# Weight splits taken off GpSimd and a second block's products shifted by one unit, in the experts of a hybrid decoder layer

## The chip, the cores and the metric

The kernel is one program on one core of a Trainium2 chip. The metric is the device time of one execution in microseconds (us); lower is better. TensorE is written PE in the profile, its weight load PEld, VectorE DVE, ScalarE ACT, GpSimd POOL, SyncE SP. [...]

## The reference, cut to what matters

One layer: attention and a short convolution, a mixture of experts, and an embedding gate. The change lies in the experts. 2048 tokens each choose one of 4 groups by a router, and two of the 8 experts in that group:

```python
def expert_block(args):
    xblk, e = args
    hdn = jax.nn.silu(xblk @ w_gate[e]) * (xblk @ w_up[e])
    return hdn @ w_down[e]
```

A token's two results, weighted, are added to its row. `w_gate` and `w_up` are 1024 x 512 for each of the 32 experts, `w_down` 512 x 1024, all float32.

## The kernel before, in words

*Stages.* `build` runs the input projection, the attention, the output projection with the routing (`mix_out`), the experts (`far_experts`, for tokens past an expert's first 192, then `experts`), and `finish`. Products are made of two float32r parts of each operand: `split` (line 59) writes hi = cast of src on ScalarE (line 65), and lo = src - hi (line 66), on VectorE unless another engine is named. `mm3` (lines 73 to 75) adds hi·hi, hi·lo and lo·hi.

*Weights as a ring.* An expert's weights are 12 units of 128 x 1024: 0 to 3 of `w_gate`, 4 to 7 of `w_up` (two halves of 256 columns, two units each), 8 to 11 of `w_down`. SP loads them into 12 raw buffers in turn (`unit_loads`, line 749). `split_unit` splits the next one into one of 10 pairs `uh`, `ul`; with `pool=True` lo is made on GpSimd. In `block` the call `free` says that the place of a unit is done with, and splits the next in line there (`next_unit`, line 764), which also issues the next load.

*An expert.* Loop over 32 experts, `block(e, more)`: the first 128 tokens ("first block"), and, under a branch on the expert's count, 64 more ("second block", `more`). `prods(j, 0)` multiplies unit j with the first block (6 products of 512 columns, or 12 of 256); `prods(j, 1)` with the second, whose hi and lo rows stand side by side as 128 rows (4 or 8 products, lines 1286 and 1287). `first(j)` and `others(j)` call them and do what follows: after unit 3 the SiLU; after units 5 and 7 a half of the hidden layer (`hidden`: for the first block `u`, line 1300; for the second `half`, which adds its two halves of rows by a ScalarE copy in line 1251 and a VectorE addition in line 1252, and the product of line 1297, tile `sum`); a unit later its transposes on TensorE (`hidden_trans`, line 1307) and their split (`hh`, `hl`; for the second block `hs`). After units 8 and 9 the next expert's tokens are transposed (line 1230). After unit 11 `store` empties the output banks: line 1321 on ScalarE for the first block, `half` again for the second.

*Order.* The schedule is manual: each engine runs its instructions in the order in which the code issues them. The loop is, for j from 1 to 10: `first(j)`, `others(j - 1)`, `free(j in (4, 6))`; then `others(10)`, `others(11)`, `first(11)`. So two units per expert are split with lo on GpSimd, and the second block stays one unit behind the first. The transposes go into a pool of two PSUM tiles, `tr`, used in turn by all transposes of the experts. Banks are six: 0 and 1 for the gate (first and second block), 2 to 5 for `w_up` and then for the outputs.

GpSimd's queue also holds the gathers of tokens (line 1221) at an expert's head and the stores of results (lines 1323 and 1325).

Of the kernel before, what the change touches and what calls it, by code (L numbers as in the profile page):

```python
# [18 lines left out]
DRAM = bass.MemoryType.DRAM  # L19
# [11 lines left out]
EPS = 1e-6  # L31
# rows of the experts' outputs: the first 128 of each expert, then the next 64 of each;
# those past 192 go in blocks of 128 of their own
R1 = E * 128
R2 = R1 + E * 64
FAR = 192
# units of weights on chip, as loaded and split
NRAW, NSPLIT = 12, 10
# [3 lines left out]
# tiles of p @ w_ple_proj that wait until the experts are done  # L42
# [3 lines left out]
def row_bc(ap, n):  # L46
    """A DRAM row of n elements, read by every partition."""
    return bass.AP(tensor=ap.tensor, offset=ap.offset, ap=[[0, 128], [1, n]])


class Kernel:
# [7 lines left out]
    def split(self, hi, lo, src, lo_eng=None, hi_eng=None, later=None):  # L59
        """hi + lo = src, each of them exact in float32r; lo only noted where it is for later."""  # L60
        nc = self.nc
        if hi_eng:
            hi_eng.tensor_copy(hi, src)
        else:
            nc.scalar.activation(hi, src, AF.Copy)  # L65
        f = lambda: (lo_eng or nc.vector).tensor_tensor(lo, src, hi.bitcast(F32), op=OP.subtract)  # L66
        f() if later is None else later.append(f)

    def mm3(self, ps, terms, start=True, stop=True):
        """ps += sum of (ah + al)^T (bh + bl), al^T bl aside."""  # L70
        mm, n = self.nc.tensor.matmul, len(terms)
        for i, (ah, al, bh, bl) in enumerate(terms):
            mm(ps, ah, bh, start=(start and i == 0), stop=False)  # L73
            mm(ps, ah, bl, start=False, stop=False)  # L74
            mm(ps, al, bh, start=False, stop=(stop and i == n - 1))  # L75

    def acc(self, ps, prods):
        """ps = the sum of products."""
        for i, (l, r) in enumerate(prods):
            self.nc.tensor.matmul(ps, l, r, start=i == 0, stop=i == len(prods) - 1)  # L80

    def rsqrt_steps(self, pool, r, v):
        """r = v ** -0.5, from an integer guess and three Newton steps; stops between two of them."""
        V = self.nc.vector
        t = pool.tile([128, r.shape[1]], F32, name="rsq_t", bufs=2)
        ri = r.bitcast(I32)
        V.tensor_scalar(ri, v.bitcast(I32), 1, None, op0=OP.logical_shift_right)
        yield
        V.tensor_scalar(ri, ri, -1.0, float(0x5F3759DF), op0=OP.mult, op1=OP.add)
        for _ in range(3):  # L90
            yield
            V.scalar_tensor_tensor(t, r, -0.5, r, op0=OP.mult, op1=OP.mult)
            yield
            V.tensor_tensor(t, t, v, op=OP.mult)
            yield
            V.scalar_tensor_tensor(r, t, 1.5, r, op0=OP.add, op1=OP.mult)
# [6 lines left out]
    def rms_steps(self, pool, r, ss, n):  # L103
        """r = 1 / sqrt(ss / n + EPS), by columns."""
        v = pool.tile([128, ss.shape[1]], F32, name="rms_v", bufs=2)
        self.nc.vector.tensor_scalar(v, ss, 1.0 / n, EPS, op0=OP.mult, op1=OP.add)
        yield
        yield from self.rsqrt_steps(pool, r, v)
# [62 lines left out]
    def project(self, st):  # L171
        tc, nc, a = self.tc, self.nc, self.a
# [51 lines left out]
        # gains and taps as columns: q 0-2, kv 3-4, taps 5-16 (tap, channel tile)  # L224
# [5 lines left out]
        # rows of the rotary tables: frequency, phase in turns, phase; 64 of cosines, 64 of sines  # L230
# [8 lines left out]
        # sums of every 32nd row  # L239
# [26 lines left out]
        def up_weights():  # L266
            # tiles of 128 columns: 0-3 two heads each without rotation, 4-5 the rotated halves of four heads each
# [176 lines left out]
        def start():  # L444
            """The first tokens' way to the first columns, in the order in which they come."""
# [8 lines left out]
            later = []  # L454
# [81 lines left out]
    def rope_angles(self, f512, pi, rcol):  # L536
        """Angles within a turn, for positions pi, a row's kind given by rcol."""
# [17 lines left out]
        # a turn more or less where the first guess was a little off  # L555
# [10 lines left out]
    def attention(self, st):  # L566
# [32 lines left out]
        def scores(h, g, qi, c):  # L599
            """Scores of 128 queries and 512 keys; with the last of a row's, its softmax."""  # L600
# [70 lines left out]
        def sums(h, g):  # L671
            """1 / the softmax's sums."""
            sm = groups[h, g]["sm"] = wk.tile([128, 4], F32, name="sm")
            nc.vector.tensor_reduce(sm, groups[h, g]["rs"][:, :, :g + 1], axis=AX.X, op=OP.add)
            nc.vector.reciprocal(sm, sm)

        def sums_row(h, g):
            """The same along the free axis, on a head's partitions."""
            G, a0 = groups[h, g], heads[h]["a0"]
            q = nc.sync if (h, g) == hg[-1] else nc.gpsimd  # L680
            q.dma_start(self.rd[h, g].rearrange("(a b) -> b a", b=128), G["sm"])
            rb = G["rb"] = wk.tile([128, 512], F32, name="rb")
            q.dma_start(rb[a0:a0 + 64], self.rd[h, g].unsqueeze(0).to_broadcast([64, 512]))

        def normalise(h, g):
            """o^T of a head and 512 queries."""
# [30 lines left out]
        for n in range(len(s_seq) + lag_v):  # L717
# [5 lines left out]
            # a group's last product goes first: what comes next waits for its bank  # L723
# [12 lines left out]
    def ring(self, st):  # L736
        """Weights in units of [128, 1024]: NRAW as they come, NSPLIT split, both used in turn."""
# [13 lines left out]
    def split_unit(self, scale=None, pool=False, later=None):  # L751
        """The next unit's parts, its rows multiplied by scale."""
# [16 lines left out]
    def mix_out(self, st):  # L769
# [50 lines left out]
        # constants of the norm and of the routing; router weights, both levels side by side, hi and lo  # L820
# [31 lines left out]
        # kept: weights, expert and rank of a token's two choices  # L852
# [15 lines left out]
        def trans(t):  # L868
            """xn^T, split, two tiles of tokens side by side."""
# [12 lines left out]
        def logits(t):  # L882
            """Router logits of tiles t and t + 1, transposed; the parts of hi and lo weights below each other."""
# [14 lines left out]
        def route(t0, n):  # L898
            """The choices of n tiles of tokens, and their rows; a step at a time."""
# [13 lines left out]
            def first(hot, d, w, k):  # L913
                """The first of the zeros in d, one-hot."""
# [25 lines left out]
            # one-hot experts, ranks among an expert's tokens  # L940
# [27 lines left out]
            # places in the lists; a far token's is past their end  # L968
# [28 lines left out]
        def go(k=-1, ranks=False):  # L997
            """k steps of the routing, or all (-1); past the ranks' products only if told so."""
# [81 lines left out]
        # the last tiles' way to the lists, beside tiles of p @ w_ple_proj  # L1080
# [38 lines left out]
        # counts of tokens, and of blocks of 128 past FAR  # L1119
# [11 lines left out]
        # rows and weights of a token's two choices, nought if it is far  # L1131
# [22 lines left out]
    def ple_prep(self, wk, t, pst, keep=None):  # L1154
        """p^T of a tile, split; or only kept."""
# [27 lines left out]
    def unit_loads(self, most=NRAW):  # L1183
        """Loads of weights as far ahead as there is room."""
# [34 lines left out]
    def gather(self, e, r):  # L1219
        """The rows of an expert's first 128 tokens (r = 0) or the next 64; where there is none, a row is left."""  # L1220
# [17 lines left out]
    def experts(self, st):  # L1238
# [8 lines left out]
        def half(ps, n, out=None):  # L1247
            """The sum of the two halves' rows."""
# [6 lines left out]
        def block(e, more):  # L1255
            """An expert's first 128 rows; with more, 64 others, their hi and lo side by side."""
# [10 lines left out]
            def free(pool=False):  # L1267
                """A unit is done with: the next in line takes its place."""
                self.next_unit(pool)

            def prods(j, r):
                """Unit j's products, for the first rows (r = 0) or the others."""
# [19 lines left out]
            def hidden(f, r):  # L1292
                """The hidden layer's columns of half f, and where they go transposed."""
# [48 lines left out]
            def others(j):  # L1342
# [6 lines left out]
                if j in (6, 8):  # L1349
                    hidden_trans((j - 6) // 2, 1, U[1 - j])  # L1350
# [10 lines left out]
            # the places of the expert before's last two units, and of all but the last two of this one's  # L1361
# [3 lines left out]
            for j in range(1, 11):  # L1365
                first(j)
                if more:
                    others(j - 1)
                free(j in (4, 6))
            if more:  # L1370
                others(10)
                others(11)
            first(11)
# [16 lines left out]
    def far_experts(self, st):  # L1390
# [3 lines left out]
        # apart from where the experts start  # L1394
# [6 lines left out]
        with tc.If(nov > 0):  # L1401
            cum = wk.tile([128, E], F32, name="cum")
            V.tensor_tensor_scan(cum, self.ones[:, :E], nb, 0.0, op0=OP.mult, op1=OP.add)
            # the expert of a block
# [10 lines left out]
            # rows of the far tokens  # L1415
# [82 lines left out]
    def finish(self, st):  # L1498
# [124 lines left out]
        # sums of squares: of tile t - 2 (after the embedding) and t + 2 (before)  # L1623
# [37 lines left out]
        # the last tile in parts  # L1661
# [86 lines left out]
```

## Time and profile before

| | |
|---|---|
| three runs | 2479.6, 2488.54, 2501.54 us |
| median | 2488.54 us |
| span of the profiled execution | 2492.2 us |
| PE busy | 2313.6 us, 93% of the span |
| DVE, ACT, POOL busy | 1728.2, 1341.4, 701.6 us (69%, 54%, 28%) |
| mean granted clock of TensorE | 0.966 |

The profile is of one execution. Its times come from the hardware's records: each instruction's start and duration, the idle time before it on its engine, and the instruction on another engine whose semaphore released it. A matmul's end is modelled, so neighbouring products overlap in the rows; their starts tell how fast TensorE goes. ScalarE's and VectorE's rows are merged where equal ones follow each other ("x2").

### The profile page before, as it was taken

Reading aid. Unit: us, or ns where it says so; the run is one execution under the profiler, and the core shown is the slowest. Engines: PE = TensorE matmul, PEld = TensorE weight load, DVE = VectorE, ACT = ScalarE, POOL = GpSimd, SP = SyncE. Lnnn points to the kernel's source line nnn. Section 1 sums busy time; section 2 is a strip of 40 time slices with the busy share of each in tenths; the row PEclk is TensorE's granted clock in tenths of the full one; section 3 lists DMA queues with packets and bytes.
Section 4 is the critical chain, followed back from the end, with each engine's and each line's share of the span. In section 5 each row is a group of like instructions: output and inputs, shape, how many; then the busy total and the mean of one; then the engine's idle time right before and its main releaser. Section 6 shows DMA issues by size and latency. Waiting matters only on the chain. (4 is left out here: it accounts for less than half of the span.)

```text
span 2492.2 us, 34982 instructions
## 1 busy us (share of the span) xinstructions
PE 2313.6 (93%) x12058; PEld 1904.2 (76%) x12058; DVE 1728.2 (69%) x3007; ACT 1341.4 (54%) x2409; POOL 701.6 (28%) x671
## 2 busy tenths in 40 slices
PE   7999999989999999979997998999999999999997
PEld 5878787877787777768785777877787878787775
DVE  6746556537777777767676777667666776776887
ACT  5333333326777777742224666656656665665434
POOL 2121212122233333352333233213322232223342
PEclk9999999998999999999998998999999999999999
DMA  7363635355545444465656789778877887784562
GB/s 216 104 207 102 200 98 180 89 164 105 113 109 118 117 80 80 104 136 183 204 176 209 265 284 317 250 236 285 273 225 245 294 277 262 254 298 148 169 203 94
DMA packets 298378, 465.68 MB, mean 187 GB/s; under 512 B 28105, under 2 KB 198130, under 8 KB 298130
## 3 DMA queue, kind: packets, MB, share of 16 engines
q1 hardware_dynamic: 254304, 333.56, 44.6%
q0 software_dynamic: 36304, 105.39, 13.0%
q10 hardware_dynamic: 7522, 23.61, 2.5%
q8 instruction: 133, 2.18, 0.4%
q14 instruction: 115, 0.94, 0.1%
HBM read 369.04 MB, written 97.62 MB: 187 GB/s over the span
## 5 line engine op out<-in xcount | busy, mean ns | idle before, releaser
L66 DVE TENSOR_TENSOR ul<-raw,uh 128x1024 fp32r<-128x1024 f32 x326 | 465.7, 1446 | 189.3 <-ACT uh L65 175.5
L65 ACT ACTIVATE uh<-raw 128x1024 fp32r<-128x1024 f32 x396 | 403.3, 1052 | 85.7 <-PE bank L1286 36.8
L73 PE MATMUL bank<-uh,xh 128*128 128x256 f32 (+1 forms) x768 | 253.4, 330 | 21.1 <-ACT uh L65 12.1
L74 PE MATMUL bank<-ul,xh 128*128 128x256 f32 (+1 forms) x768 | 249.4, 325 | 3.6 <-issue 3.6
L75 PE MATMUL bank<-uh,xl 128*128 128x256 f32 (+1 forms) x768 | 248.8, 324 | 2.6 <-issue 2.6
L66 POOL TENSOR_TENSOR ul<-raw,uh 128x1024 fp32r<-128x1024 f32 x70 | 170.2, 2433 | 278.2 <-ACT uh L65 242.8
L66 DVE TENSOR_TENSOR pt<-tr,pt 128x512 fp32r<-128x512 f32 (+2 forms) x320 | 194.6, 610 | 76.5 <-ACT pt L65 73.3
L65 ACT ACTIVATE pt<-tr 128x512 fp32r<-128x512 f32 (+2 forms) x317 | 168.9, 533 | 116.5 <-PE tr L655 111.9
L634 DVE TENSOR_REDUCE mx<-s 128x1 f32<-128x512 f32 (+2 forms) x320 | 192.7, 603 | 45.5 <-PE s L631 40.1
L73 PE MATMUL mm<-xh,wh 128*128 128x512 f32 x536 | 212.2, 398 | 6.9 <-ACT xh L65 6.9
L75 PE MATMUL mm<-xh,wl 128*128 128x512 f32 x536 | 212.0, 396 | 0.0
L74 PE MATMUL mm<-xl,wh 128*128 128x512 f32 x536 | 211.8, 395 | 0.0
L666 PE MATMUL av<-pt,v 128*128 128x512 f32 (+3 forms) x640 | 207.1, 408 | 1.4 <-ACT lo L694 1.4
L643 ACT ACTIVATE P<-s,mx 128x512 f32<-128x512 f32 (+2 forms) x320 | 198.8, 622 | 11.5 <-DVE mx L639 11.5
L65 ACT ACTIVATE wh<-raw 128x1024 fp32r<-128x1024 f32 x68 | 72.0, 1060 | 219.0 <-PE mm L74 184.7
L655 PE MATMUL tr<-ident,P 128*128 128x128 f32 x1088 | 180.6, 283 | 0.0
L73 PEld LDWEIGHTS bank<-uh,xh 128*128 128x128 f32 x768 | 147.0, 191 | 38.9 <-issue 24.3
L629 PE MATMUL s<-k,q 96*128 96x512 f32 (+2 forms) x320 | 131.9, 412 | 36.2 <-DMA q<-qrd 27.3
L75 PEld LDWEIGHTS bank<-uh,xl 128*128 128x128 f32 x768 | 147.2, 192 | 18.4 <-issue 6.2
L74 PEld LDWEIGHTS bank<-ul,xh 128*128 128x128 f32 x768 | 147.4, 192 | 14.0 <-issue 1.1
L66 DVE TENSOR_TENSOR xl<-tr,xh 128x512 fp32r<-128x512 f32 x160 | 106.0, 684 | 70.8 <-ACT xh L65 69.6
L655 PEld LDWEIGHTS tr<-ident,P 128*128 128x128 f32 x1088 | 134.7, 146 | 24.9 <-issue 2.0
(371 smaller groups left out, 5587.5 us busy)
## 6 DMA issues: line engine op xcount, KB each, us to landing
raw<-in_w_gate_dram SPq DMA_DIRECT2D x128, 512.0 KB
raw<-in_w_up_dram SPq DMA_DIRECT2D x128, 512.0 KB
raw<-in_w_down_dram SPq DMA_DIRECT2D x128, 512.0 KB
raw<-in_w_in_dram SPq DMA_DIRECT2D x68, 512.0 KB
yd<-y POOLq DMA_DIRECT2D x32, 512.0 KB
xr<-in_x_dram SPq DMA_DIRECT2D x16, 512.0 KB
kd<-stg POOLq DMA_DIRECT2D x16, 512.0 KB
vd<-stg POOLq DMA_DIRECT2D x16, 512.0 KB
```

What stands on the lines that cost most here:

```text
L65: nc.scalar.activation(hi, src, AF.Copy)
L66: f = lambda: (lo_eng or nc.vector).tensor_tensor(lo, src, hi.bitcast(F32), op=OP.subtract)
L73: mm(ps, ah, bh, start=(start and i == 0), stop=False)
L74: mm(ps, ah, bl, start=False, stop=False)
L75: mm(ps, al, bh, start=False, stop=(stop and i == n - 1))
L629: mm(s, qh, k[:, 0, :w], start=True, stop=False)
L634: nc.vector.tensor_reduce(mx[:, c:c + 1], s, axis=AX.X, op=OP.max, negate=(g == 0))
L643: nc.scalar.activation(G["P"][qi][:, j * 512:j * 512 + s.shape[1]], s, AF.Exp, bias=nm, accum_out=G["rs"][:, qi, j:j + 1])
L655: nc.tensor.transpose(ps[:, jj], G["P"][qi][:, j * 128:j * 128 + 128], self.ident)
L666: mm(G["av"][:, q0:], heads[h]["v"][:, j], G["pt"][jq][:, hl, jj, q0:], start=(j == 0 and hl == 0), stop=(j == 4 * g + 3 and hl == 1))
```

## The change

`free` no longer takes `pool`, so every weight split of the experts has lo on VectorE. The second block's transposes leave `others`: the first pair is issued before `others(7)`, after `first(8)`, and the second before `others(8)`, which itself, with `others(9)`, comes one unit later. `first(11)` moves ahead of `others(9)`. With one block only, the order of products is as it was. Comments were also taken out, which moves the lines by 12; this is not shown.

```diff
-            def free(pool=False):
-                self.next_unit(pool)
+            def free():
+                self.next_unit()
...
                 if j in (5, 7):
                     U[-j] = hidden((j - 5) // 2, 1)
-                if j in (6, 8):
-                    hidden_trans((j - 6) // 2, 1, U[1 - j])
                 if j == 11:
                     store(1)
...
             free()
             free()
             first(0)
-            for j in range(1, 11):
+            for j in range(1, 9):
                 first(j)
                 if more:
+                    if j == 8:
+                        hidden_trans(0, 1, U[-5])
                     others(j - 1)
-                free(j in (4, 6))
+                free()
+            first(9)
             if more:
+                first(10)
+                hidden_trans(1, 1, U[-7])
+                others(8)
+                free()
+                first(11)
+                others(9)
+                free()
                 others(10)
                 others(11)
-            first(11)
+            else:
+                free()
+                first(10)
+                free()
+                first(11)
```

On TensorE, in an expert with a second block, between the products of unit 6 with the second block (`xs`, the first two rows) and those of unit 7 with it (the last two); `u` and `sum` are the hidden halves of the first and second block, `xg` the next expert's tokens:

```order
 L1286 MATMUL bank_13781<-uh_10187,xs 128x256
 L1287 MATMUL bank_13781<-ul_10188,xs 128x256
-L1307 MATMUL tr<-ident,sum 128x64 x2
 L73 MATMUL bank_13778<-uh_10191,hh 128x512
 L74 MATMUL bank_13778<-ul_10192,hh 128x512
@@ -5175,4 +5174,5 @@
 L1307 MATMUL tr<-ident,u 128x128 x2
 L1230 MATMUL tr<-ident,xg_12721 128x128 x4
+L1307 MATMUL tr<-ident,sum 128x64 x2
 L1286 MATMUL bank_13781<-uh_10189,xs 128x256
 L1287 MATMUL bank_13781<-ul_10190,xs 128x256
```

The second block's two transposes move behind unit 8's products with the first block, its second transposes and the first four of the next expert's tokens.

On VectorE, in the same expert, from the SiLU's sum of the second block (`sil`) to the second half of the hidden layer; `ul` are weight splits:

```order
 L66 TENSOR_TENSOR ul_10180<-raw_10170,uh_10179 128x1024
 L1252 TENSOR_TENSOR sil_13797<-bank_13777,lo 64x512
+L66 TENSOR_TENSOR ul_10182<-raw_10171,uh_10181 128x1024
 L1300 TENSOR_TENSOR u<-bank_13778,sil 128x256
 L66 TENSOR_TENSOR ul_10184<-raw_10160,uh_10183 128x1024
@@ -1818,9 +1819,10 @@
 L1252 TENSOR_TENSOR sum<-bank_13779,lo 64x256
 L1297 TENSOR_TENSOR sum<-sum,sil_13797 64x256
-L1300 TENSOR_TENSOR u<-bank_13780,sil 128x256
-L66 TENSOR_TENSOR hs<-tr,hs 128x2x64
+L66 TENSOR_TENSOR ul_10186<-raw_10161,uh_10185 128x1024
+L1300 TENSOR_TENSOR u<-bank_13780,sil 128x256
```

Two weight splits join VectorE's queue, each right in front of a `u` of line 1300.

On VectorE, in an expert with one block only, about the same two halves of the hidden layer:

```order
 L66 TENSOR_TENSOR ul_10180<-raw_10170,uh_10179 128x1024
+L66 TENSOR_TENSOR ul_10182<-raw_10171,uh_10181 128x1024
 L1300 TENSOR_TENSOR u<-bank_13778,sil 128x256
 L66 TENSOR_TENSOR ul_10184<-raw_10160,uh_10183 128x1024
 L66 TENSOR_TENSOR hl<-tr,hh 128x256
+L66 TENSOR_TENSOR ul_10186<-raw_10161,uh_10185 128x1024
 L1300 TENSOR_TENSOR u<-bank_13780,sil 128x256
 L66 TENSOR_TENSOR ul_10188<-raw_10162,uh_10187 128x1024
```

Here too each new split stands right in front of a `u`.

## Rows read from the trace of the kernel before

**Rows 1.** Head of the page.

```profile
span 2492.2 us, 34982 instructions
```

**Rows 2.** Busy time of the expert stage: start:end, length, each engine, PEclk, DMA share, GB/s.

```profile
1360.00:2255.00 895.00, 829.26 (x4673) 700.52 (x4674) 639.68 (x680) 563.27 (x761) 245.40 (x155) 0.96 0.79 268
```

**Rows 3.** TensorE's waits in the expert stage: us in total, times, longest.

```profile
PE tr L1307 <- DVE sum L1297: 30.0, 16, 2.2
...
PE bank L75 <- DVE hl L66: 2.7, 15, 0.2
```

**Rows 4.** Groups, expert stage: busy, mean ns, idle before; last row: ns min/median/max.

```profile
L66 DVE TENSOR_TENSOR ul<-raw,uh 128x1024 fp32r<-128x1024 f32 x315 | 445.6, 1432 | 182.9 <-ACT uh L65 169.2 <-DMA raw<-in_w_up_dram 4.9 <-DMA raw<-in_w_down_dram 4.5
...
L66 POOL TENSOR_TENSOR ul<-raw,uh 128x1024 fp32r<-128x1024 f32 x63 | 152.4, 2420 | 272.0 <-ACT uh L65 242.8 <-DMA raw<-in_w_down_dram 16.4 <-PE bank L74 9.0
...
L1297 DVE TENSOR_TENSOR sum<-sum,sil 64x256 f32<-64x256 f32 x32 | 34.9, 1090 | 1.1
...
L1297 DVE TENSOR_TENSOR sum<-sum,sil x32: 416/419/2124, 1384.2 to 2242.7; 64x256 f32<-64x256 f32 x32
```

**Rows 5.** Timeline of an expert with a second block: start us, us, engine, [idle <- releaser].

```profile
1648.26 0.42 DVE L1300 TENSOR_TENSOR u<-bank,sil 128x256 f32<-128x256 f32 x1
...
1648.77 1.99 ACT L65 ACTIVATE uh<-raw 128x1024 fp32r<-128x1024 f32 x2
...
1649.90 2.39 POOL L66 TENSOR_TENSOR ul<-raw,uh 128x1024 fp32r<-128x1024 f32 x1 [8.70 <-ACT uh L65]
...
1650.44 0.38 PE L1307 MATMUL tr<-ident,u 128*128 128x128 f32 x2
...
1650.80 2.57 DVE L66 TENSOR_TENSOR ul<-raw,uh 128x1024 fp32r<-128x1024 f32 x1 [2.11 <-ACT uh L65]
...
1653.27 2.35 POOL L66 TENSOR_TENSOR ul<-raw,uh 128x1024 fp32r<-128x1024 f32 x1 [0.98 <-ACT uh L65]
...
1654.07 1.83 DVE L1297 TENSOR_TENSOR sum<-sum,sil 64x256 f32<-64x256 f32 x1
...
1656.05 0.30 PE L1307 MATMUL tr<-ident,sum 64*128 64x64 f32 x2 [1.91 <-DVE sum L1297]
```

**Rows 6.** Timeline of the same expert, a little later.

```profile
1657.64 1.23 DVE L66 TENSOR_TENSOR ul<-raw,uh 128x1024 fp32r<-128x1024 f32 x1 [0.65 <-ACT uh L65]
1657.79 0.38 PE L1307 MATMUL tr<-ident,u 128*128 128x128 f32 x2
...
1658.21 0.38 ACT L65 ACTIVATE hh<-tr 128x256 fp32r<-128x256 f32 x1 [0.59 <-PE tr L1307]
1658.36 0.36 PE L1286 MATMUL bank<-uh,xs 128*128 128x256 f32 x1
...
1658.79 0.42 DVE L66 TENSOR_TENSOR hl<-tr,hh 128x256 fp32r<-128x256 f32 x1
```

**Rows 7.** Busy time in 4 us behind such waits, 2 of 15; PEclk third from last.

```profile
1656.05:1660.05 4.00, 4.00 (x25) 3.52 (x26) 2.77 (x6) 2.67 (x6) 0.00 (x0) 1.00 0.66 201
1689.16:1693.16 4.00, 4.00 (x15) 3.24 (x16) 1.86 (x4) 1.61 (x3) 0.00 (x0) 0.57 0.66 226
```

**Rows 8.** Sums over two neighbouring experts with a second block, 1635.18 to 1668.28 to 1702.89.

```profile
sum 33.10, PE 31.19 PEld 26.64 DVE 22.50 ACT 19.72 POOL 8.58; mean PE 7.80 PEld 6.66 DVE 5.62 ACT 4.93 POOL 2.14
...
sum 34.61, PE 32.69 PEld 28.05 DVE 22.58 ACT 19.61 POOL 6.97; mean PE 8.17 PEld 7.01 DVE 5.65 ACT 4.90 POOL 1.74
```

**Rows 9.** Timeline of an expert with one block only.

```profile
2042.81 2.95 ACT L65 ACTIVATE uh<-raw 128x1024 fp32r<-128x1024 f32 x3
...
2046.39 0.38 PE L1307 MATMUL tr<-ident,u 128*128 128x128 f32 x2
```

**Rows 10.** Timeline of the last expert, which has a second block.

```profile
2238.72 0.30 PE L1307 MATMUL tr<-ident,sum 64*128 64x64 f32 x2 [0.49 <-DVE sum L1297]
```

**Rows 11.** Head of a one-block expert: its first product (timeline), and the stretch behind it (busy time).

```profile
2200.17 0.47 PE L73 MATMUL bank<-uh,xh 128*128 128x512 f32 x1 [1.66 <-ACT y L1321]
...
2200.20:2203.60 3.40, 3.40 (x15) 2.78 (x16) 2.98 (x3) 2.50 (x4) 0.00 (x0) 1.00 0.71 213
```

## The prediction

> **What bounds the kernel now.** I read the span first [rows 1], then the busy time of the expert stage alone [rows 2], then TensorE's waits in that stage [rows 3], and last one expert in order of time. The stage lasts 895 us. TensorE is busy 829.26 us of it, VectorE 639.68, ScalarE 563.27, so TensorE is the bound there, at a mean granted clock of 0.96 [rows 2]. Its largest wait is for VectorE's product in line 1297: 30.0 us in 16 waits [rows 3]. Sixteen is the number of experts with a second block ("two-block experts"; the other 16 are "one-block experts").
>
> The reader should see how that wait comes about. At 1653.27 GpSimd starts a weight split of 2.35 us; at 1654.07 VectorE starts line 1297 and needs 1.83 us for it; TensorE, which wants that product transposed next, stands 1.91 us [rows 5]. Just before, another GpSimd split (1649.90 to 1652.29) holds VectorE's own split to 2.57 us [rows 5], where the same split takes 1.23 us with GpSimd quiet [rows 6]. In the last expert no GpSimd split lies beside line 1297, and the same wait is only 0.49 us [rows 10]. So the wait is made by GpSimd beside VectorE.
>
> It costs more than itself. In the 4 us after the 15 long waits of this kind the granted clock is 1.00 five times and 0.57 to 0.69 ten times (one of each shown) [rows 7]. An expert whose clock stays up takes 33.10 us, the next one, whose clock falls, 34.61 [rows 8]: 1.51 us for the fall. After a wait of 1.66 us at the head of a one-block expert the clock stayed at 1.00 [rows 11].
>
> **The change part by part.**
>
> *Splits off GpSimd.* 63 splits of 2420 ns leave GpSimd [rows 4] and become VectorE splits of 1.23 us [rows 6]: 63 x 1.23 = +77 us of VectorE work. Against this, VectorE's 315 splits average 1432 ns [rows 4], 0.20 above 1.23, which is 64 us, and its 32 products of line 1297 average 1090 ns [rows 4], against a median of 419 [rows 4], which is 21 us. Together 85 us go and 77 come: VectorE's total stays near 632 us, below TensorE's 829. It does not become the bound, but its order does.
>
> [...] By offloading alone, taking the splits back would add the 77 us to VectorE; by the rows above it comes out 8 us lighter. [...]
>
> *The first new wait.* In the pass j = 4 of the loop the freed place takes a new unit, and its split now stands on VectorE in front of u, line 1300 (second order fence). Before, u ran at 1648.26 with nothing ahead of it [rows 5]. TensorE needs u for the transposes of line 1307. ScalarE's two casts start at 1648.77 and take 1.99 together [rows 5], so the first is done at about 1649.8; the split then runs to 1651.0, u to 1651.4, and with the 0.15 us that lie between line 1297's end (1655.90) and TensorE's start (1656.05) [rows 5] TensorE can transpose at 1651.55 instead of 1650.44 [rows 5]. A wait of 1.1 us, sixteen times. It comes with the split alone, whatever the order of TensorE's products. The split of j = 6, moved likewise, stands in front of the second u; by the same steps that u ends near 1656.0, and its transposes come at 1656.7, so it costs nothing in a two-block expert.
>
> *The second block's first transposes one unit later.* They now follow the first block's second transposes and the next expert's four (first order fence). Their data is long there: with 1.1 us of delay and 0.42 us for line 1297 it ends about 1654.2, and TensorE reaches the transposes near 1657.3. But the pool of transposed tiles has two buffers, and the one they take is that of the first block's transposes just two tiles back. It comes free when VectorE's hl has read it. In the rows the chain is: transposes at 1657.79, ScalarE's hh at 1658.21, VectorE's hl from 1658.79 to 1659.21 [rows 6], then 0.15: 1.57 us after the transposes began. TensorE has filled only until 1658.36, where its next products begin now (0.57 us) [rows 6]. The new wait is 1.0 us; with VectorE idle when hh ends (1658.59) it would be 0.8. The product of unit 7 that could have covered it comes behind the waiting transposes, not ahead.
>
> *Sum for a two-block expert.* 1.1 + 1.0 come, 1.9 goes: 0.2 worse. The short waits for hl that the old splits cause (2.7 us in 15) [rows 3] go too, which brings it near even. I take 0, between -0.5 and +0.5: 0 us in all, between -8 and +8.
>
> *The clock.* The two new waits lie some 6 us apart (ending near 1651.5 and 1658.3) and each is shorter than the 1.66 after which the clock held [rows 11]. I count all ten falls as saved: 10 x 1.51 = -15 us. Bounds: nothing saved, and -15.
>
> *One-block experts.* There too the split comes in front of u. Three casts start at 2042.81 and take 2.95 [rows 9], so the middle one ends near 2044.8; split to 2046.1, u to 2046.5, transposes at 2046.7 instead of 2046.39 [rows 9]: 0.3 us. A second u, one unit pair later, stands behind a moved split in the same way; its gain and loss against GpSimd's hindrance I set at nothing. +0.3 x 16 = +5 us; bounds 0 and +10 (0.6 each).
>
> *The last products one unit later.* first(11) now runs before others(9), so the second block's outputs are the last to leave. Its evacuation (two ScalarE casts and two VectorE additions in turn) ends later than the copies of line 1321 that were last before, and holds the next expert's xs split back. The xs products come some 3 us into the next expert, which covers it: 0; at worst 0.5 us in each of the at most 15 transitions between two-block experts, +7. Two units per two-block expert are also freed some 2.5 us later, so SP issues their successors' loads later; those units are needed half an expert afterwards, so this is hidden. GpSimd's queue keeps only gathers and stores, which start no later.
>
> Sum: 0 - 15 + 5 = -10 us, on the profiled span of 2492.2 [rows 1]: 2482. The profiled execution is known by its span alone; the median of the runs, 2488.5, lies 3.7 below it, so the forecast is 2478. The bounds add to -23 (-8, -15, 0) and +25 (8, 0, 10, 7).
>
> **The rivals.**
>
> *Both new waits are hidden* (VectorE reaches u and hl sooner than I place them, since nothing holds it any more). Then the whole 30 us of waits [rows 3] and the 15 us of clock go: -45, about 2444. For it: the wait of 0.49 in rows 10, where line 1297 is undisturbed. Against it: the order of VectorE's queue and the cast's end at 1649.8, both fixed. The point where it decides: each new wait under 0.5 us.
>
> *The waits move and take the clock along.* If the two new waits are 0.5 us longer together than the old one, and the clock falls behind them as often as before, two-block experts lose 8 us, one-block experts up to 10, and nothing is saved: +18, about 2506, slower than before. For it: two waits in an expert where there was one, and new ones in the one-block experts; against it: the shorter wait that left the clock at 1.00 [rows 11]. It decides from a clock saving under 13 us with the upper bounds of the rest.
>
> *The change does as it says, but only the clock is in doubt.* Waits even, falls as many as before: +5, about 2493, no difference.
>
> Beside these, the gaps at the heads of some one-block experts, as the 1.66 us of rows 11, may shift by some microseconds in all, either way, for reasons that the change does not touch.
>
> **How the numbers follow.** A measurement of this kernel tells about 1%, 25 us. My forecast 0.6 (2478, own range 2466 to 2490), both hidden 0.17 (2444), waits and clock move 0.11 (2506), only the clock in doubt 0.12 (2493). Faster by over 1% (under 2463.7): the second case and a tail of the first, 0.22. Slower by over 1% (over 2513.4): the upper part of the third and a tail of the fourth, 0.07. The rest, 0.71, is within 1%. The range, 2448 to 2504, leaves out the lower half of the second case and the upper half of the third.
>
> **What would show it.** Right: no wait of TensorE on line 1297; instead 16 waits near 1.1 us of line 1307's transposes of u on line 1300, 16 near 1.0 us of its transposes of sum on hl, smaller ones in one-block experts; VectorE's splits at 1.23 us; two-block experts at 33 us throughout and a granted clock in the stage of 0.98. Wrong: two-block experts near 31 us (no new waits), or clock rows near 0.6 behind the new waits.

## The result and the profile after

| | before | after |
|---|---|---|
| median of 20 runs each, taken side by side | 2491.07 us | 2474.34 us |
| ratio, 95% interval | | 0.994 [0.9923, 0.9957] |
| span of the profiled execution | 2492.2 us | 2485.7 us |
| two-block experts, 14 whole ones | 479.6 us | 461.2 us |
| one-block experts, 16 | 320.1 us | 320.1 us |
| idle time at the experts' heads | 21.1 us | 25.2 us |

The change is faster by about 15 us (2491.07 x 0.006): the interval leaves out 1, but the gain is within the 1% that the prediction calls no difference. 2478 was forecast. The lengths of experts are worked out from the timeline: from the start of an expert's first product or transpose to that of the next expert's, less the idle time in front of the latter, which is the last row of the table. The first and the last expert, both two-block, are left out. The three rows add to -14.3 us (-18.4 + 0 + 4.1), so within the expert stage the whole gain lies in the two-block experts. The two spans differ by 6.5 us only: in the profiled execution of after the stretch ahead of the first expert, which the change does not touch, is 7.0 us longer (TensorE's first row of the experts at 1369.63 instead of 1362.62 us; in the profiles of all runs it lies between 1355 and 1374).

The head of the page of after, and the busy time of its expert stage (columns as in [rows 2]):

```profile
span 2485.7 us, 34965 instructions
```
```profile
1369.00:2246.00 877.00, 817.03 (x4667) 688.74 (x4668) 619.98 (x736) 564.17 (x757) 96.74 (x92) 0.98 0.80 272
```

The granted clock, which the profile gives as a share of full speed, went from 0.96 [rows 2] to 0.98, GpSimd from 245 us to 97, and VectorE did not become busier by taking the splits: 620 us against 640. The groups of the stage answer to [rows 4]:

```profile
L66 DVE TENSOR_TENSOR ul<-raw,uh 128x1024 fp32r<-128x1024 f32 x381 | 458.6, 1223 | 190.5 <-ACT uh L65 180.8 <-DMA raw<-in_w_up_dram 3.3 <-DMA raw<-in_w_down_dram 1.1
...
L1297 DVE TENSOR_TENSOR sum<-sum,sil 64x256 f32<-64x256 f32 x32 | 13.3, 417 | 1.1
```

Of the 66 splits that are more here, 63 come from GpSimd; the other three are there because this row was taken over a longer stretch (1350 to 2255) than [rows 4]. The 66 cost only 13.0 us (445.6 to 458.6), the 63 alone 9.3, since one takes 1223 ns instead of 1432; line 1297 fell from 34.9 us to 13.3.

Not all of VectorE's work had been slowed. In the kernel before, between its slow split and line 1297, and beside the GpSimd split that started at 1653.27 [rows 5], VectorE ran these two:

```profile
1653.29 0.41 DVE L66 TENSOR_TENSOR hl<-tr,hh 128x256 fp32r<-128x256 f32 x1
1653.63 0.41 DVE L1252 TENSOR_TENSOR sum<-bank,lo 64x256 f32<-64x256 f32 x1
```

They took what they take with GpSimd quiet (0.42 us each). They read one operand from PSUM (`tr`, `bank`); line 1297 and the weight splits read both from SBUF. It is so in the whole expert stage of before: line 1297 took 1.79 to 2.12 us in the 15 cases beside a GpSimd split and 0.42 in the other 17, and 47 weight splits that lay beside one for 1.49 us or more took 2.57 to 2.67 us instead of 1.23, while `u` of line 1300, which reads `bank`, took 0.40 to 0.42 in all 64, half of them beside one.

TensorE's waits in the stage answer to [rows 3]:

```profile
PE tr L1307 <- DVE u L1300: 20.7, 36, 1.1
PE bank L73 <- ACT uh L65: 14.2, 5, 3.4
PE tr L1307 <- DVE hl L66: 8.7, 15, 0.6
...
PE tr L1357 <- PE bank L1287: 3.3, 8, 0.5
```

The 30.0 us for line 1297 are gone. In their place stand a wait for `u` and one for `hl`, as forecast, and a third that was not: 0.36 to 0.47 us, eight times, at the head of a two-block expert that follows another (line 1357 is 1359 of before). The 36 waits for `u` are one of 0.81 to 1.15 us in each two-block expert, one of 0.24 in each one-block expert, and four of 0.47 to 0.85 in one-block experts that follow a two-block one. Waits for ScalarE's weight casts (line 65) at the heads of one-block experts were there before, too (4, of 12.1 us). In one two-block expert the first two look like this in the timeline, which answers to [rows 5, 6]:

```profile
1616.25 1.99 ACT L65 ACTIVATE uh<-raw 128x1024 fp32r<-128x1024 f32 x2
1617.33 1.23 DVE L66 TENSOR_TENSOR ul<-raw,uh 128x1024 fp32r<-128x1024 f32 x1 [1.65 <-ACT uh L65]
1618.47 0.42 DVE L1300 TENSOR_TENSOR u<-bank,sil 128x256 f32<-128x256 f32 x1
...
1618.94 0.44 PE L1307 MATMUL tr<-ident,u 128*128 128x128 f32 x2 [0.86 <-DVE u L1300]
...
1623.93 0.38 PE L1307 MATMUL tr<-ident,u 128*128 128x128 f32 x2
1624.35 0.38 ACT L65 ACTIVATE hh<-tr 128x256 fp32r<-128x256 f32 x1 [0.67 <-PE tr L1307]
1624.86 0.42 DVE L66 TENSOR_TENSOR hl<-tr,hh 128x256 fp32r<-128x256 f32 x1
1625.33 0.34 PE L1307 MATMUL tr<-ident,sum 64*128 64x64 f32 x2 [0.58 <-DVE hl L66]
```

The split stands in front of `u` (1617.33, 1618.47), TensorE starts when `u` ends; 6.4 us later the second block's transposes start when `hl` has read the tile that they need. All 14 whole two-block experts take 32.8 to 33.1 us; in the kernel before four took 33.1 to 33.3 and ten 34.6 to 35.0.

### The profile page after: what moved, and what is told of

Read it like the earlier page. It is cut to its first block, busy times and chain, and to the rows that moved or that the text cites. A ratio compares the mean times of both kernels' runs of the same rounds, so it can differ in the third digit from the quotient of the medians.

```text
span 2485.7 us, 34965 instructions
## 1 busy us (share of the span) xinstructions
PE 2305.6 (93%) x12058; PEld 1895.8 (76%) x12058; DVE 1710.8 (69%) x3070; ACT 1344.8 (54%) x2409; POOL 550.8 (22%) x608
## 5 line engine op out<-in xcount | busy, mean ns | idle before, releaser
L66 DVE TENSOR_TENSOR ul<-raw,uh 128x1024 fp32r<-128x1024 f32 x389 | 475.0, 1241 | 190.7 <-ACT uh L65 180.8
L1325 POOL DMA_DIRECT2D yd<-y x32 | 18.3, 571 | 678.1 <-ACT y L1321 641.1
```

## The experiments

The theory behind all of them: GpSimd's splits slow VectorE (2.57 us for a weight split instead of 1.23, 1.83 for line 1297 instead of 0.42) and so make the wait of 1.9 us, and a wait of that length takes the clock along in most cases (to 0.57 to 0.69 behind ten of 15 in the kernel before); taking the splits away is the gain, and the shift of the second block's products costs some of it. The rivals stand in each expectation. The table shows every run; lengths of experts as above. An expert counts as one with a fall of the clock when the granted clock behind its wait is below 1.00; all of these take over 1 us longer than the others of the run.

| run | ratio, 95% interval | two-block experts, 14 | with a fall of the clock | one-block, sum |
|---|---|---|---|---|
| before | 1 | 33.1–33.3 and 34.6–35.0, sum 479.6 | 10 | 320.1 |
| the change | 0.994 [0.9923, 0.9957] | 32.8–33.1, 461.2 | 0 | 320.1 |
| splits only | 0.9895 [0.9867, 0.9924] | 32.1–32.3, 450.9 | 0 | 317.8 |
| order only | 0.9989 [0.9968, 1.001] | 32.7–32.9 and 34.3–34.5, 466.1 | 4 | 318.3 |
| one split | 0.985 [0.982, 0.9881] | 31.6–31.8, 443.2 | 0 | 319.3 |
| u first, old order | 0.9801 [0.9774, 0.9827] | 31.0–31.2, 435.7 | 0 | 307.2 |
| u first, new order | 0.9864 [0.9833, 0.9895] | 31.7–31.9, 445.3 | 0 | 306.1 |
| tail back | 0.9926 [0.9901, 0.995] | 32.8–33.2, 461.0 | 0 | 317.0 |
| four additions | 0.995 [0.9931, 0.9969] | 33.1–33.2 and 34.7–34.9, 480.0 | 10 | 310.2 |
| three additions | 0.9878 [0.9846, 0.9909] | 32.3–32.5, 453.9 | 0 | 311.9 |
| transposes swapped | one run, no ratio | 32.8–33.1, 460.8 | 0 | 324.9 |

**Splits only.** The kernel before, with no split on GpSimd:

```diff
-                free(j in (4, 6))
+                free()
```

> The kernel before with one part of the change: every expert split on VectorE, the order of products as before. Theory (the change traded one long wait for shorter ones of the same sum and gained by the clock, which no longer falls): line 1297 takes 0.42 us and TensorE's wait on it is under 0.3 us; the wait of the transposes for u stays at 0.86; no wait on hl or at the next expert's head, since these came with the order. Two-block experts near 32.0 us, none with a fall of the clock; about 30 us less than before, ratio 0.988, so better than the whole change. Rival 1 (the shifted order is what hides the wait, and the splits off GpSimd alone only load VectorE): the wait on line 1297 stays above 1 us and the ratio is 0.995 or more.

Measured 0.9895. TensorE's waits in the stage:

```profile
PE tr L1307 <- DVE u L1300: 17.6, 32, 0.9
```

No wait for line 1297, none for `hl`, only the one for `u`, and no fall of the clock in a two-block expert. This part alone is worth more than the whole change: the two intervals just touch, and the two-block experts take 450.9 us against 461.2.

**Order only.** The kernel after, with the two splits on GpSimd again:

```diff
-            def free():
-                self.next_unit()
+            def free(pool=False):
+                self.next_unit(pool)
...
-                free()
+                free(j in (4, 6))
```

> The other part alone: the shifted order, with the splits of j = 4 and 6 on GpSimd as before. Theory: line 1297 still takes about 1.9 us beside GpSimd, but nothing waits for it now; instead the second u, behind it on VectorE, keeps its transposes waiting about 1.0 us, and the second block's transposes wait 0.6 to 1.0 us for hl. Two waits again under 1.7 us each, so the clock does not fall: ratio 0.994, like the whole change. Rival 2 (only the splits off GpSimd gain, the order is idle): a wait near 1.9 us remains in one piece, the clock still falls behind it, ratio 1.00.

Measured 0.9989: the theory's 0.994 was missed, and 1.00 is the rival's number, though not by the rival's wait of 1.9 us in one piece, which is gone. The waits, and the product of line 1297:

```profile
PE tr L1307 <- DVE u L1300: 13.1, 16, 1.1
PE tr L1307 <- DVE hl L66: 8.9, 15, 0.6
PE bank L75 <- DVE hl L66: 5.8, 15, 1.0
```
```profile
L1297 DVE TENSOR_TENSOR sum<-sum,sil 64x256 f32<-64x256 f32 x32 | 35.3, 1103 | 1.1
```

Line 1297 is as slow as before (1103 ns), but TensorE no longer waits for it, since its transposes come later: the shift does hide the old wait. In a two-block expert it waits instead for the second `u`, queued behind line 1297, and for `hl` ahead of the second block's transposes: 13.1 and 8.9 us, 22.0 against the 30.0 of before [rows 3]. The third row lies in the one-block experts alone, as its 2.7 us of before do: four of them, each behind a two-block expert, now wait 0.92 to 0.98 us. The clock still fell in four of the 14 experts, though no wait in them is above 1.1 us. One of the four, in the timeline and in the busy time behind:

```profile
1649.90 0.44 PE L1307 MATMUL tr<-ident,u 128*128 128x128 f32 x2 [0.82 <-DVE u L1300]
...
1651.37 0.34 PE L1307 MATMUL tr<-ident,sum 64*128 64x64 f32 x2 [0.59 <-DVE hl L66]
```
```profile
1653.00:1657.00 4.00, 4.00 (x17) 3.25 (x17) 2.17 (x4) 1.93 (x3) 0.00 (x0) 0.70 0.37 119
```

Here the second wait follows 1.5 us behind the first, and the clock behind both is 0.70 (0.57 to 0.61 in the 4 us right behind the second wait in the four experts, 1.00 in the other ten); in the changed kernel the two lie some six apart, and none was followed by a fall. That the distance decides was not tried by itself. The profiles show more gain than the runs: the two-block experts are 13.5 us shorter in sum, with 5.5 us more at the heads, and the spans are 9.7 apart (2492.2 and 2482.5), the medians only 3.6. Most of this is which executions were profiled: that of this run was 2 us shorter than its median (2484.24 against 2486.25), and that of before some 4 us longer than its own, by an estimate (its span and the 1.7 us that lie between span and time in the other runs).

**One split.** The kernel before, with only the split of j = 6 on VectorE:

```diff
-                free(j in (4, 6))
+                free(j == 4)
```

> The kernel before with only the split of j = 6 moved to VectorE (the one beside line 1297); that of j = 4 stays on GpSimd, the order as before. Theory: u of line 1300 has no split in front of it and TensorE does not wait for it in two-block experts; the wait on line 1297 is 0.5 us, as in the last expert of before; no falls. Two-block experts near 31.7 us; 35 us less than before, ratio 0.986. Rival 1: wait on line 1297 above 1 us, ratio 0.995 or more.

Measured 0.985, better than with both splits moved; the intervals overlap a little, the two-block experts take 443.2 us against 450.9.

```profile
PE tr L1307 <- DVE sum L1297: 7.9, 16, 0.5
...
PE tr L1307 <- DVE u L1300: 4.3, 16, 0.3
```
```profile
L1297 DVE TENSOR_TENSOR sum<-sum,sil 64x256 f32<-64x256 f32 x32 | 13.4, 418 | 1.1
```

The split of j = 6 alone made line 1297 slow (418 ns without it). With the other still on GpSimd, `u` has nothing in front of it in a two-block expert, and the wait for line 1297 is 0.5 us.

**u first, old order.** The kernel before, all splits on VectorE, the lo parts of the two moved ones issued behind `u` of line 1300 (with the loads that follow them):

```diff
-    def next_unit(self, pool=False):
+    def next_unit(self, pool=False, later=None):
...
-        self.split_unit(self.gcol[:, k:k + 1] if k >= 0 else None, pool)
-        self.unit_loads()
+        self.split_unit(self.gcol[:, k:k + 1] if k >= 0 else None, pool, later)
+        if later is None:
+            self.unit_loads()
...
                     U[j] = hidden((j - 5) // 2, 0)
+                    for f in held:
+                        f()
+                    held.clear()
+                    self.unit_loads()
...
-                free(j in (4, 6))
+                self.next_unit(later=held if j in (4, 6) else None)
```

> The order of before, all splits on VectorE, and the two moved splits issued behind the u of line 1300 that they stood in front of (with the load that reuses their raw buffer). Theory: neither the wait on line 1297 nor that for u is left; two-block experts near 31.1 us, one-block experts near 19.0, no falls: 33 us of waits and 15 us of clock, ratio 0.981. Rival 3 (behind these waits stands another limit, as the loads of weights or the branches at the experts' heads): two-block experts above 32 us or longer one-block experts, ratio 0.987 or more.

Measured 0.9801, 2442.16 us: the best of all, ahead of both kernels. The timeline of a two-block expert (lines moved by one):

```profile
1643.99 0.42 DVE L1298 TENSOR_TENSOR sum<-sum,sil 64x256 f32<-64x256 f32 x1
1644.33 0.41 DVE L1301 TENSOR_TENSOR u<-bank,sil 128x256 f32<-128x256 f32 x1
1644.66 1.21 DVE L66 TENSOR_TENSOR ul<-raw,uh 128x1024 fp32r<-128x1024 f32 x1
...
1645.16 0.33 PE L1308 MATMUL tr<-ident,sum 64*128 64x64 f32 x2
...
1646.91 0.38 PE L1308 MATMUL tr<-ident,u 128*128 128x128 f32 x2
```

Both hidden halves are done before TensorE comes for them, the split follows, and no row of TensorE names a wait for `u`, `sum` or `hl`. One-block experts gain as well: 307.2 us against 317.8 with splits only.

**u first, new order**, and **tail back**: the same edit in the kernel after; and the kernel after with `first(11)` last again:

```diff
-                first(11)
                 others(9)
                 free()
                 others(10)
                 others(11)
+                first(11)
```

> The changed kernel, with the two splits that it took off GpSimd issued behind u of line 1300 instead of ahead of it, as in the run with u first in the old order. Theory (the split ahead of u makes the waits for u, 20.7 us in the changed kernel; the shifted order has a price of its own, some 12 us, by its waits for hl and at the next expert's head): the waits for u go, the others stay; ratio to the kernel before 0.985 (about 2454 us), 12 us behind the run with u first in the old order. Rival 1 (the shift costs only what its own waits show, 12 us, but these shrink too once VectorE is ahead): 0.981, even with that run. Rival 2 (the waits only move on to the next one): 0.992, little better than the changed kernel.

> The changed kernel, with first(11) last in a two-block expert again, so that only the transposes and the products of units 7 and 8 stay shifted. Theory (the unforeseen wait of 0.36 to 0.47 us at the head of the next two-block expert comes from the second block's outputs being emptied last): those 8 waits go, 3 to 4 us, the waits for u (0.86) and hl (0.58) stay; ratio 0.992. Rival (the head's wait comes from VectorE's heavier queue at the expert's end, whichever output is last): the waits stay, 0.994.

Measured 0.9864 and 0.9926. The waits of the first, in the stage (lines moved by one and by six):

```profile
PE tr L1308 <- DVE hl L66: 8.8, 15, 0.6
...
PE tr L1363 <- PE bank L1288: 3.3, 8, 0.5
```

The waits for `u` are gone and the other two stand as they did, and the interval leaves out both rivals' numbers (0.981, 0.992), so the theory holds: the shifted order costs 0.0063 of the ratio beside u first (16 us), and 0.0045 beside splits only (11 us); its two rows show 12.1 us. With the tail back, the wait at the head is gone from the rows and those for `u` and `hl` stay (18.2 and 8.7 us), as the theory says; 0.9926 against 0.994 is too near to be told apart by the runs. So the order of the last products makes the third wait. It makes the four longer waits for `u` in one-block experts, too: with the tail back there are 32 waits for `u` instead of 36, each one-block expert has only that of 0.24 us, and these experts take 317.0 us in sum instead of 320.1. The row of the wait at the head names TensorE's own last product as the releaser; which buffer stands behind that was not tried.

**Four additions, three additions.** The run with u first in the old order, and VectorE held up on purpose, with no GpSimd split anywhere. The additions work on a tile that nothing else reads:

```diff
+                    if f == 0:
+                        for _ in range(4):
+                            V.tensor_tensor(pad, pad, pad, op=OP.add)
                     V.tensor_tensor(u, u, sl1[:, fs], op=OP.mult)
```

> The run with u first in the old order, and in each two-block expert four additions of 128x512 on VectorE, which compute nothing needed, ahead of the first product of line 1297 (some 2.5 us in all; line 1297 had 0.6 us to spare there). TensorE then waits about 1.9 us there, as in the kernel before, with GpSimd making no split. Theory (the clock falls behind a wait of this length, whoever makes it): 16 waits of 1.9 are 30 us, falls behind some ten of them 15 more; ratio 0.999 (2487 us), half clock in the stretches behind the waits, two-block experts of 33 and of 34.5 us. Rival (the falls came with GpSimd's work beside the others, not with the wait): 0.993 (2472 us), all two-block experts about 33 us, clock 1.00 behind the waits.

> The same with three additions (some 1.9 us): TensorE waits about 1.25 us in each two-block expert. Theory (a wait as short as this leaves the clock up, as I counted for the new waits of the changed kernel): 16 waits are 20 us, no falls; ratio 0.989 (2462 us), two-block experts near 32.4 us. Rival (a wait of 1.25 us is enough for falls): 0.995 (2477 us), some two-block experts near 34 us.

Measured 0.995 and 0.9878. With three the theory's number (0.989) lies in the interval and the rival's does not. With four the interval leaves out the theory's 0.999 and, barely, the rival's 0.993, so the rows must decide. With four additions, one two-block expert, and the busy time in the 4 us behind two of the 16 waits (PEclk third from last):

```profile
1610.02 2.85 DVE L1302 TENSOR_TENSOR pad<-pad 128x512 f32<-128x512 f32 x4
1612.79 0.41 DVE L1303 TENSOR_TENSOR sum<-sum,sil 64x256 f32<-64x256 f32 x1
...
1613.35 0.31 PE L1313 MATMUL tr<-ident,sum 64*128 64x64 f32 x2 [1.98 <-DVE sum L1303]
```
```profile
1613.35:1617.35 4.00, 4.00 (x25) 3.52 (x26) 3.83 (x7) 2.68 (x6) 0.00 (x0) 1.00 0.29 101
1646.53:1650.53 4.00, 4.00 (x16) 3.38 (x17) 3.17 (x5) 1.64 (x4) 0.00 (x0) 0.60 0.25 92
```

With three, the same two places:

```profile
1613.11 0.31 PE L1313 MATMUL tr<-ident,sum 64*128 64x64 f32 x2 [1.25 <-DVE sum L1303]
```
```profile
1613.11:1617.11 4.00, 4.00 (x25) 3.52 (x26) 3.83 (x7) 2.68 (x6) 0.00 (x0) 1.00 0.38 117
1645.56:1649.56 4.00, 4.00 (x25) 3.53 (x26) 3.83 (x7) 2.67 (x6) 0.00 (x0) 1.00 0.38 115
```

Sixteen waits of 1.93 to 2.04 us were followed by a clock of 0.57 to 0.71 eleven times and of 1.00 five times; sixteen of 1.20 to 1.31 us by 1.00 every time. With four additions the two-block experts read like those of before, ten with a fall and four without, though GpSimd does nothing beside them (0.00 us busy in all sixteen stretches). So the falls need no GpSimd: they came with the wait. Whether GpSimd adds to them was not tried apart.

The runs agree less sharply than the rows. The two medians are 19.4 us apart (2483.74 and 2464.32), the two rows of waits 11.6 (31.7 and 20.1, below), so 8 us are left for the falls, where ten at 1.5 would be 15. In the profiled executions it is nearer: the spans are 23.4 us apart (2486.1 and 2462.7), which leaves 11.8. The one with four additions was longer than its median (2487.82 us), and of the twelve executions the longest had the lowest mean clock (2490.28 us at 0.962) and the shortest the highest (2474.02 at 0.968). That fits a number of falls that differs from one execution to the next; it was counted in the profiled one only.

```profile
PE tr L1313 <- DVE sum L1303: 31.7, 16, 2.0
```
```profile
PE tr L1313 <- DVE sum L1303: 20.1, 16, 1.3
```

Nor does the length of a wait decide alone. At the heads of one-block experts TensorE also waits for longer. In the kernels before and after the 13 longest of these waits took 2.15 to 3.94 us, and the clock in the 4 us behind was 0.50 to 0.68 nine times, but 1.00 behind those of 2.58, 2.76 and 3.04 us (before) and 2.52 us (after). Behind one of 3.43 with three additions the products kept starting every 0.23 to 0.24 us; behind the one of 3.58 they started 0.42 to 0.43 us apart.

**Transposes swapped.** The kernel after, with the second block's first transposes ahead of the first block's second ones:

```diff
+                if j == 8 and more:
+                    hidden_trans(0, 1, U[-5])
                 if j in (6, 8):
                     hidden_trans((j - 6) // 2, 0, U[j - 1])
...
-                    if j == 8:
-                        hidden_trans(0, 1, U[-5])
```

> The changed kernel, with the second block's first transposes issued ahead of the first block's second ones and of the next expert's four, instead of behind them. Theory (a transposed tile waits for whatever lies two tiles back in the pool of two): the 15 waits for hl go, since hs of those transposes is then the nearer neighbour; the next expert's four transposes (line 1230) now lie two tiles behind them and wait for hs, some 0.6 to 0.9 us, 15 or 16 times; two-block experts stay near 32.9 us, the profiled span near 2486. Rival (the wait belongs to VectorE's delay alone, whichever tile it is): the wait for hl stays where it is, or goes without a successor and two-block experts fall to 32.3 us.

One run; the waits in the stage:

```profile
PE tr L1307 <- DVE u L1300: 19.9, 35, 1.2
...
PE tr L1230 <- DVE hs L66: 7.0, 15, 0.5
```

The wait for `hl` went and a like one for `hs` came, two tiles behind it, as the theory of the two buffers has it; at 0.5 us it is a little shorter than I had said (0.6 to 0.9), and the experts stay at 32.8 to 33.1 us. The span, 2471.9 us, is not 2486, but that difference lies ahead of the experts, whose first row stands at 1355.06 us instead of 1369.63.

## Why the prediction was right

The mechanism was right, and the time (2474 against 2478) with it, but that it came so near is partly luck. The sum forecast -10 us and the ratio gives -15; two smaller terms were off in opposite directions; and the forecast started from a median of before of 2488.5, which was 2491.07 in the runs taken side by side.

*Splits off GpSimd.* Right in direction: VectorE was to become 8 us lighter; by the two groups, with 63 splits, it is +9.3 - 21.6 = -12.3 us. (The stage as a whole shows 20 us less, 639.68 to 619.98, but over a shorter stretch.)

*The first new wait.* Right at 1.1 us. The row says 0.86, but a wait counts from the modelled end of the product before it, which overlaps the next start when nothing waits. The experts' lengths tell the price: 32.93 against 31.83 with u first in the new order, 32.2 against 31.1 in the old one, 1.1 us both times. Counted in the same way the old wait cost 33.1 - 31.1 = 2.0 us, not 1.9.

*The second block's first transposes one unit later.* The mechanism was right, as the swapped run shows, the size not: 1.0 us was taken, and the lengths give 0.7 (32.93 - 32.2, and 31.83 - 31.1). The chain that I set at 1.57 us after the transposes took 1.40 (1623.93 to 1625.33), as VectorE was idle when `hh` ended: the 0.8 that the prediction named as its other end was the nearer one.

*Sum for a two-block expert.* 1.1 + 0.7 - 2.0 = -0.2 us; the lengths give 33.1 to 32.9. Forecast 0, within its 0.5. One of its reasons was misread: the short waits for `hl` (2.7 us in 15) lie, by the timeline, all in one-block experts. Without them the forecast was +0.2; the smaller 0.7 of the term above brought it to -0.2.

*The clock.* Right: all ten falls in two-block experts are gone, 10 x 1.5 = 15 us of the 18.4 that these experts lost. It was the term with most doubt, and the two runs with additions show why it came out so: each of the new waits, of at most 1.15 us, is shorter than those of 1.20 to 1.31 us behind which the clock never fell in sixteen cases. The order-only run warns that shorter ones close together can still be followed by falls, in four of 14 experts (in one of them 0.82 and 0.59 us, 1.5 us apart).

*One-block experts.* Wrong by 5 us: forecast +5, measured 0. By the starts of TensorE's rows the split ahead of the first `u` costs 0.26 us (the transposes start 0.38 us behind the product before them, 0.12 in the kernel before), near the 0.3 of the forecast. That ahead of the second `u` costs 0.41 (0.64 and 0.23), which I set at nothing. Against both stands what GpSimd's splits had cost in these experts, which I also set at nothing. The waits for `hl` are part of it: 15 of 0.34 us by the starts (0.57 against 0.23). U first, with neither cost, shows all of it: 13 us less than before (320.1 to 307.2), and 18.2 to 18.4 us in an expert with no fall or other stall, against 18.9 to 19.2 both before and after. Not all of these 0.8 us are accounted for by rows.

*The last products one unit later.* The step that failed, though its bound held. I wrote that the xs products, 3 us into the next expert, cover the later outputs: "0; at worst 0.5 us in each of the at most 15 transitions". The transposes of xs themselves wait, 0.36 to 0.47 us in eight transitions (there are eight, not 15), 3.3 us; and the four longer waits for `u` in one-block experts behind two-block ones, 2.8 us, come with this order, too, as the run with the tail back shows. The head waits were not forecast and the one-block experts' +5 did not come, and these two errors cancel nearly; the rest of the difference is the two-block experts, whose lengths fell by 18.4 us where 15 was forecast.

The rivals: both waits hidden (2444) did not come by this change, but u first in the old order is that case, at 2442 (13 us of its gain are in the one-block experts). What I named as deciding against it, the order of VectorE's queue, made the wait for `u`; that for `hl` came from the order of TensorE's transposes, as it stays when `u` goes first in the new order. The waits did not take the clock along: it was 1.00 in the 4 us behind each of them.

## What to carry to other kernels

Work given to GpSimd may free nothing on VectorE: here VectorE's operations with both operands in SBUF took up to five times as long beside it (line 1297 1.79 to 2.12 us instead of 0.42, a weight split 2.57 to 2.67 instead of 1.23), those with one in PSUM did not (0.40 to 0.42 us beside it, 0.40 to 0.43 without). Look at VectorE's duration per shape with and without the neighbour before counting the offload as a gain. When work moves into an in-order queue, ask what stands behind it: the same splits cost 1.1 us per two-block expert in front of `u` and nothing behind it. And price a wait by the length of the loop body in two kernels, not by the idle time alone, and by what the clock does behind it.

## What the runs showed of the hardware

A granted clock of 1.00 behind all sixteen waits of 1.20 to 1.31 us, and of 0.57 to 0.71 behind eleven of sixteen waits of 1.93 to 2.04, in kernels that differ by one addition, and 1.5 to 1.7 us lost per fall (34.6 against 33.1 before, 34.8 against 33.1 with the additions). Length is not all: of the 13 longest waits, of 2.15 to 3.94 us, at the heads of one-block experts (before and after) nine were followed by 0.50 to 0.68, but four of 2.52 to 3.04 us by 1.00. Pairs of waits of at most 1.1 us, 1.5 us apart, were followed by falls in four of 14 experts of the order-only run, which I had not expected. And 63 splits on GpSimd lengthened what VectorE ran beside them by more than VectorE needs to do them itself: 315 x (1432 - 1223 ns) + 32 x (1090 - 417 ns) = 87 us, against 63 x 1.223 = 77. Of VectorE's operations beside a GpSimd split only those with both operands in SBUF were lengthened (1.79 to 2.12 us instead of 0.42 for line 1297, 2.57 to 2.67 instead of 1.23 for a weight split); those with one operand in PSUM (`u`, `hl`, the sum of line 1252) were not: 0.40 to 0.42 us beside one, 0.40 to 0.43 without.
